# Four wide expert places become places of at most 96 tokens, computed in float32 on four 32-column quarters of the array

## The chip, the core and the metric

The kernel runs on one core of one Trainium2 chip. A core has TensorE (PE: matmuls, with weight loads listed apart as PEld), VectorE (DVE), ScalarE (ACT), GpSimd (POOL) and SyncE (SP, which here issues the transfers), each with its own instruction queue, and 16 DMA engines that bring data from HBM into the core's memory. The metric is the device time of one execution in microseconds (us). Before the change it is 1349.42 us, the median of 3 runs (1347.88 to 1350.05).

## The reference

A trunk of two layers on 256 tokens of width 1024. Each layer has a mixer (spatial gating, a recurrence and sparse attention) and a channel mixer; the first layer's channel mixer is dense, the second's has eight experts, of which each token uses two. The change touches the experts alone:

```python
def moe_swiglu(x, router_w, router_b, w1, w3, w2):
    logits = (x @ router_w + router_b).astype(jnp.float32)
    top_v, top_i = lax.top_k(logits, TOP_K)          # TOP_K = 2 of 8
    top_p = jax.nn.softmax(top_v, axis=-1)
    gate = jnp.sum(jax.nn.one_hot(top_i, N_EXPERTS) * top_p[..., None], axis=-2)
    out = jnp.zeros_like(x)
    for e in range(N_EXPERTS):
        out = out + gate[..., e:e + 1] * swiglu(x, w1[e], w3[e], w2[e])
    return out
```

with `swiglu(x, w1, w3, w2) = (silu(x @ w1) * (x @ w3)) @ w2`, w1 and w3 of 1024 x 2816, w2 of 2816 x 1024, all float32. All weights of all eight experts are read: 8 x 3 x 1024 x 2816 x 4 bytes, in 264 pieces of 1 MB.

## The kernel before

**Places.** The experts are worked through in eight places, in the order `SLOTS = "BSBBSBBS"`. The router's counts decide at run time which expert goes into which place: the three experts with the fewest tokens go to the narrow S places (at most `SCAP` = 64 tokens), the others to the wide B places (at most `CAP` = 128). The expert `FIRST` always has the first place, so that its weights can be fetched before the router has decided. Should some expert have more tokens than its place holds (`cmi` > 0), a second pass over all experts runs under `tc.If`.

**One place.** `gather` brings the tokens of two places into the core's layout by matmuls with a one-hot matrix `oh` (L1634). Then the 2816 hidden columns are done in chunks of 512 (five, and one of 256). For a chunk, `up` computes x @ w1 and x @ w3 into PSUM tiles A and B, over eight k-blocks of 128; `down` applies silu, gate and product (L1718, L1719), transposes the result (tile D, L342) and multiplies with w2 into tile O. `finish` runs a chunk's `down` after the next chunk's `up` in the program's order. After the last chunk `combine` scales O, splits it, and (every second place) adds two places' results into `h` by matmuls with `oT` and VectorE adds (L1768).

**Wide and narrow.** A B place computes in the format fp32r, where a matmul has to be split to keep the precision: each weight block `raw` is split into `hi` (ScalarE, L415) and `lo` (VectorE, L416), the tokens likewise into `mxh` and `mxl`, and a product takes three matmuls (`mm3`, L425) on the full array, 128 tokens as the stationary operand and 512 weight columns as the moving one. An S place uses plain float32 matmuls without any split, directly from `raw`: 64 tokens take half the array's columns, and two matmuls stand side by side, w1 on the one half and w3 on the other (`up_s`, L1703), or the two halves of w2's columns (`down`).

**Order and buffers.** The weights come in pieces of 1 MB (`raw`, L311) through a ring of 11 buffers (six, three and two of three pools, `ringm`, L1511). SP issues the transfers in one order, and each waits until its buffer has been read: in a B place by the splits, in an S place by the matmuls. Instructions are put in order per engine by a scheduler before the run; no engine leaves its order.

**Quarters elsewhere.** Float32 matmuls on 32-column quarters stand in the kernel already, in the compression of the attention keys (out tile A, stationary `pr`, L1049): four matmuls with different stationary blocks and different weights, 128 columns each, side by side.

Of the kernel before, what the change touches and what calls it, by code (L numbers as in the profile page):

```python
# [9 lines left out]
FP = mybir.dt.float32  # L10
# [8 lines left out]
P = 128  # L19
S = 256  # L20
# [20 lines left out]
    "GggGGGGgGgggg",  # L41
)
NE, NM, NL, NX = 6, 3, 2, 2
SLOTS = "BSBBSBBS"
FIRST = 1
SCAP = 64
EARLY = set("zs LW a eP eN eX KR Bp Kp kp kk tmp AK kr sg LI U2 L2 L4 S hs hid gc gl hr par".split())

# [18 lines left out]
def consts():  # L67
    p = np.arange(P)
    c = np.arange(P)
    same = lambda n: (p[:, None] // n) == (c[None, :] // n)  # L70
    f = {}
    f["ident"] = np.eye(P)
    f["head2"] = (p[:, None] // 64 == np.arange(2)[None, :])
    f["blk1"] = same(64)
    d = p % 64
    f["cneg"] = np.where(c[None, :] <= p[:, None], 0.0, NEG)
    f["tri"] = p[:, None] <= c[None, :]
    f["stri"] = p[:, None] < c[None, :]
# [12 lines left out]
    f["cmpn"] = np.where(ok, 0.0, NEG).reshape(P, 32)  # L91
    f["stack"] = (p % 32)[:, None] == np.arange(32)[None, :]
    f["hsel"] = (p // 16)[:, None] == np.arange(8)[None, :]
    f["iota"] = np.broadcast_to(c[None, :], (P, P))
    f["iota8"] = np.broadcast_to(np.arange(8)[None, :], (P, 8))
    f["key0"] = np.broadcast_to(np.where(np.arange(E) == FIRST, 1e6, np.arange(E))[None, :], (P, E))
    n_s = SLOTS.count("S")
    rank = {"S": iter(range(n_s)), "B": iter([E - 1] + list(range(n_s, E - 1)))}
    f["rslot"] = np.broadcast_to(np.array([next(rank[k]) for k in SLOTS])[None, :], (P, E))
    f["scan"] = np.broadcast_to((np.arange(S) % 64 != 0)[None, :], (P, S))  # L100
    inv = (1.0 / (np.float32(500000.0) ** (np.arange(0, 16, 2, dtype=np.float32) / np.float32(16)))).astype(np.float32)
    f["inv"] = np.where(d < 16, inv[d % 8], 0.0)[:, None]
    f["cm"] = (d < 16)[:, None]
    f["cm1"] = (d >= 16)[:, None]
    f["sg"] = np.where(d < 8, -1.0, np.where(d < 16, 1.0, 0.0))[:, None]
    off, o, parts = {}, 0, []
    for k in KEEP + tuple(k for k in f if k not in KEEP):
        v = f[k]
        v = np.asarray(v, np.float32)
        off[k] = (o, v.shape[1])  # L110
        o += v.shape[1]
        parts.append(v)
    return np.ascontiguousarray(np.concatenate(parts, 1)), off
# [232 lines left out]
def trunk(ctx: ExitStack, tc: tile.TileContext, A, out):  # L346
# [1257 lines left out]
    with tc.issue_after(behind):  # L1604
        quarter(0, 1)
    cap = mo.tile([P, 8], FP, name="cap")
    V.tensor_scalar(cap, rank, SLOTS.count("S") - 0.5, float(CAP - SCAP), op0=OP.is_gt, op1=OP.mult)
    V.tensor_scalar(cap, cap, float(SCAP), None, op0=OP.add)
    cmax = mo.tile([P, 1], FP, name="cmax")
    V.tensor_sub(lt[:, 0, :], cnt, cap)  # L1610
    V.tensor_reduce(cmax, lt[:, 0, :], axis=AX.X, op=OP.max)
# [22 lines left out]
    def gather(e0, kinds, pos, gate):  # L1634
# [8 lines left out]
        for e in range(2):  # L1643
            pool = late_p[0] if gathered[0] % 3 == 2 else mo2
            gathered[0] += 1
            if kinds[e] == "S":
                xs.append(pool.tile([P, 8, SCAP], FP, tag="mxh", name="xs"))
                continue
            xs.append([pool.tile([P, 8, P], FR, tag=tag, name=tag) for tag in ("mxh", "mxl")])
        for k in range(0, 8, 2):  # L1650
            for v, src in enumerate((hh_, hl_)):
                p = ps("D", (2, 2, P))
                for j in range(2):
                    for t in range(2):
                        mm(p[:, j], src[:, t, (k + j) * P:(k + j + 1) * P], oh[:, t], j == 0 and t == 0, t == 1)
                if v == 0 and k == 0:
                    first_mm.append(TE.last)
                for e in range(2):
                    if kinds[e] == "B":
                        SC.copy(xs[e][v][:, k:k + 2, :], p[:, :, e, :])  # L1660
                    elif v == 0:
                        SC.copy(xs[e][:, k:k + 2, :], p[:, :, e, :SCAP])
                    else:
                        V.tensor_add(xs[e][:, k:k + 2, :], xs[e][:, k:k + 2, :], p[:, :, e, :SCAP])
        po = ps("D", (2, 2, P))
        for t in range(2):
            for e in range(2):
# [35 lines left out]
    def up_s(st, n, x):  # L1703
# [6 lines left out]
                    mm(p[o:o + SCAP, :n], x[:, k, :], u[:, (k - k0) * n:(k - k0 + 1) * n], k == 0, k == 7)  # L1710
        return [p[0:SCAP, :n], p[SCAP:, :n]]

    dlast = []

    def down(st, kind, y, gs, n, a, b, first, last):
        w = SCAP if kind == "S" else P
        hd = mo2.tile([P, 512], FP, tag="hd", name="hd")[0:w]
        SC.activation(hd[:, :n], a, AF.Silu, scale=gs[0:w, 1:2])  # L1718
        V.tensor_mul(hd[:, :n], hd[:, :n], b)  # L1719
        nf = n // P  # L1720
        p = ps("D", (4, w))
        for f in range(nf):
            TE.transpose(p[:, f, :], hd[:, f * P:(f + 1) * P], ident[0:w, 0:w])
        if kind == "S":
            dt = mo2.tile([P, 4, SCAP], FP, tag="dh", name="ds")
            SC.copy(dt[:, :nf, :], p[:, :nf, :])
            for f in range(nf):
                u = st.next(ringm)
                for j in range(2):
# [11 lines left out]
    def combine(cell):  # L1741
# [3 lines left out]
        else:  # L1745
            if not late_p:
                spare.close()
                late_p.append(ctx.enter_context(tc.tile_pool(name="late", bufs=1, side="right")))
            yh, yl = (late_p[0].tile([P, D], FR, tag="y" + tag, name="y" + tag) for tag in ("hi", "lo"))
        for j, yj in enumerate(y):  # L1750
            s_ = slice(j * 512, (j + 1) * 512)
            SC.activation(yh[:, s_], yj, AF.Copy, scale=gs[:, 0:1])
            V.scalar_tensor_tensor(yl[:, s_], yj, gs[:, 0:1], yh[:, s_].bitcast(FP), op0=OP.mult, op1=OP.subtract)  # L1753
        if kind == "S":
            o_ = lambda j: slice(j * SCAP, (j + 1) * SCAP)
            parts = [lambda t, j, w=w: (oT[o_(j), t, :], w[o_(j), 0:512]) for w in (yh, yl)]
        else:
            parts = [lambda t, j, w=w: (oT[:, t, :], w[:, j * 512:(j + 1) * 512]) for w in (yh, yl)]
        if e % 2 == 0:
            held[:] = parts  # L1760
            return
# [10 lines left out]
    def experts(st, kinds, pos, gate):  # L1772
        prev = None
        for e, kind in enumerate(kinds):
# [4 lines left out]
            for f in range(0, DFF, NB):  # L1779
                n = min(NB, DFF - f)  # L1780
                with ExitStack() as first:
                    if first_mm[1:] == [] and e == f == 0:
                        for i in late[0], pair[0][2]:
                            first.enter_context(tc.issue_after(i))
                    a, b = (up_s if kind == "S" else up)(st, n, x)
                if prev:
                    finish(st, *prev)
                prev = (cell, n, a, b, f == 0, f + NB >= DFF)
# [26 lines left out]
    with tc.If(cv > 0):  # L1815
        V.tensor_sub(pos, pos, cap[:, None, :].to_broadcast([P, 2, 8]))
        experts(Halves(SY, A["moe"]), "B" * E, pos, gate)
        ple(1, pj, mo2, us, True, gB)


# [16 lines left out]
```

## Time and profile before

| | |
|---|---|
| time, median of 3 runs | 1349.42 us |
| the profiled execution | 1350.0 us, its span 1348.1 us |
| PE / DVE / ACT busy | 1306.3 / 890.8 / 737.4 us |
| expert stage (first matmul of the first place to the last combine) | about 603 to 1312 us of the span |
| mean granted TensorE clock | 0.986 of full speed |

The span runs from the first to the last instruction on the engines. "Busy" for PE counts matmuls whose ends are modelled, so neighbours overlap: a matmul's cost in a stream is the distance between starts, not its listed length. A line number in the profile is a line of the kernel file; matmuls all carry L339 (transposes L342), so they are told apart by the tiles they write and read.

### The profile page before, as it was taken

To read this page: it belongs to the slowest core of one execution; us is meant where nothing else is said; L and a number is where in the kernel's file an instruction comes from. 1 tells how busy PE (TensorE), PEld (TensorE's weight loads), DVE (VectorE), ACT (ScalarE), POOL (GpSimd) and SP (SyncE) were. 2 spreads that over 40 slices of the span, in tenths; PEclk is the share of its full clock that TensorE was granted. 3 is DMA by queue.
4 is the path that set the end of the run, shared out by engine and by line. 5 is a ranking of instruction groups with operands and counts; after the bars stand their busy time and mean duration, and the time that the engine had idled before them with its cause. 6 is when DMAs were issued, how large, how long until landed. Compare 5 with 4: busy or idle time off the path is not lost. (4 is left out here: it accounts for less than half of the span.)

```text
span 1348.1 us, 23186 instructions
## 1 busy us (share of the span) xinstructions
PE 1306.3 (97%) x8993; PEld 1020.9 (76%) x8993; DVE 890.8 (66%) x1452; ACT 737.4 (55%) x1161; POOL 63.3 (5%) x99
## 2 busy tenths in 40 slices
PE   8999999999999999999999999999999999999996
PEld 7998789999978898788863478888744788786345
DVE  5856876555587656878961188898622888896126
ACT  6434665444467235658851367787512777785124
POOL 3510000000000220000000000000000000000000
PEclk9899999999999999989999999999999999999998
DMA  8434046555563245466988999999999999899990
GB/s 292 126 110 160 2 134 211 190 190 189 190 217 98 86 131 187 174 246 256 372 340 366 419 419 419 377 369 358 336 380 419 419 419 419 316 386 355 416 381 34
DMA packets 64938, 367.59 MB, mean 273 GB/s; under 512 B 8254, under 2 KB 9206, under 8 KB 30518
## 3 DMA queue, kind: packets, MB, share of 16 engines
q1 hardware_dynamic: 63862, 365.13, 71.4%
q8 instruction: 72, 1.18, 0.4%
q0 software_dynamic: 960, 0.92, 0.3%
q14 instruction: 44, 0.36, 0.1%
HBM read 364.05 MB, written 1.05 MB: 271 GB/s over the span
## 5 line engine op out<-in xcount | busy, mean ns | idle before, releaser
L416 DVE TENSOR_TENSOR lo<-raw,hi 128x1024 fp32r<-128x1024 f32 x400 | 475.2, 1223 | 108.7 <-ACT hi L415 103.2
L415 ACT CAST hi<-raw 128x1024 fp32r<-128x1024 f32 x400 | 412.0, 1052 | 162.1 <-PE O L339 48.6
L339 PE MATMUL A<-raw,xs 128*64 128x512 f32 (+1 forms) x576 | 124.2, 562 | 0.0
L586 ACT CAST hi<-raw 128x512 fp32r<-128x512 f32 (+1 forms) x128 | 69.5, 594 | 79.3 <-PE zps L339 44.5
L1719 DVE TENSOR_TENSOR hd<-hd,A 64x512 f32<-64x512 f32 (+1 forms) x18 | 11.6, 645 | 140.9 <-ACT hd L1718 140.8
L587 DVE TENSOR_TENSOR lo<-raw,hi 128x512 fp32r<-128x512 f32 (+1 forms) x128 | 84.5, 692 | 22.9 <-ACT hi L586 22.5
L339 PE MATMUL O<-xl,hi 128*128 128x256 f32 x352 | 98.5, 280 | 0.1
L339 PE MATMUL O<-xh,hi 128*128 128x256 f32 x352 | 98.5, 280 | 0.0
L339 PE MATMUL O<-xh,lo 128*128 128x256 f32 x352 | 98.1, 279 | 0.0
L1718 ACT ACTIVATE hd<-A,gs 128x512 f32<-128x512 f32 (+3 forms) x48 | 31.2, 650 | 111.4 <-PE A L339 111.4
L339 PE MATMUL B<-hi,mxh 128*128 128x512 f32 (+1 forms) x240 | 90.7, 378 | 1.2 <-ACT hi L415 1.0
L339 PE MATMUL A<-lo,mxh 128*128 128x512 f32 (+1 forms) x240 | 91.1, 380 | 0.1
L339 PE MATMUL A<-hi,mxh 128*128 128x512 f32 (+1 forms) x240 | 90.9, 379 | 0.3 <-ACT hi L415 0.2
L339 PE MATMUL B<-lo,mxh 128*128 128x512 f32 (+1 forms) x240 | 90.4, 376 | 0.0
L339 PE MATMUL A<-hi,mxl 128*128 128x512 f32 (+1 forms) x240 | 89.7, 374 | 0.0
L339 PE MATMUL B<-hi,mxl 128*128 128x512 f32 (+1 forms) x240 | 89.7, 374 | 0.0
L339 PE MATMUL O<-lo,dh 128*128 128x512 f32 x220 | 88.2, 401 | 0.3 <-DVE lo L416 0.3
L339 PEld LDWEIGHTS A<-raw,xs 128*64 128x64 f32 x576 | 39.6, 136 | 64.5 <-issue 58.8
L339 PE MATMUL O<-hi,dl 128*128 128x512 f32 x220 | 86.0, 393 | 0.0
L339 PE MATMUL zps<-xh,hi 128*128 128x256 f32 x256 | 75.7, 299 | 6.6 <-DVE zr L792 5.5
L339 PE MATMUL zps<-xh,lo 128*128 128x256 f32 x256 | 73.8, 289 | 0.4 <-DVE lo L587 0.4
L339 PE MATMUL zps<-xl,hi 128*128 128x256 f32 x256 | 73.4, 288 | 0.0
(490 smaller groups left out, 2635.4 us busy)
## 6 DMA issues: line engine op xcount, KB each, us to landing
raw<-in_moe_dram SPq DMA_DIRECT2D x263, 1024.0 KB, 8.1
raw<-in_dense_dram SPq DMA_DIRECT2D x140, 512.0 KB, 3.5
raw<-in_aux_dram SPq DMA_DIRECT2D x5, 1024.0 KB, 17.2
raw<-in_dense_dram SPq DMA_DIRECT2D x8, 280.0 KB, 2.8
small<-in_small_dram SPq DMA_DIRECT2D x2, 576.0 KB, 6.0
xT<-in_xT_dram SPq DMA_DIRECT2D x2, 512.0 KB, 4.1
h<-in_x_dram SPq DMA_DIRECT2D x2, 512.0 KB, 7.7
raw<-in_moe_dram SPq DMA_DIRECT2D x2, 512.0 KB, 16.3
```

The lines of the kernel that those rows point to most:

```text
L339: self.last = self.eng.matmul(*a, **k).ins
L415: SC.copy(hi[:, :n], src)
L416: V.tensor_sub(lo[:, :n], src, hi[:, :n].bitcast(FP))
L586: SC.copy(hi[:, s_], src[:, s_])
L587: (GP if self.early else V).tensor_sub(lo[:, s_], src[:, s_], hi[:, s_].bitcast(FP))
L1718: SC.activation(hd[:, :n], a, AF.Silu, scale=gs[0:w, 1:2])
L1719: V.tensor_mul(hd[:, :n], hd[:, :n], b)
```

## The change

`SLOTS` becomes `"MSMBSMMS"`. An M place holds at most 96 tokens and computes in float32 without splits. Its 96 tokens are three blocks of 32, and 32 tokens take a quarter of the array's columns. `thirds` works on two k-blocks at a time: for each of them a round of four quarter matmuls puts the three token blocks times w1 on quarters 0 to 2 and the third token block times w3 on quarter 3 (PSUM tile `pa`); a third round puts the first two token blocks times w3 on quarters 0 and 1 for the first k-block and on quarters 2 and 3 for the second (tile `pb`). The two halves of `pb` are added afterwards (`folded`: a ScalarE copy and a VectorE sum of 64 rows). `down` does the same with the two halves of w2's columns. Experts go to places by rank: the three with the fewest tokens to S, the next three and `FIRST` to M, the one with the most to the remaining B. The pass for overflowing places gets a second repetition.

```diff
-SLOTS = "BSBBSBBS"
+SLOTS = "MSMBSMMS"
 FIRST = 1
+WIDTH = {"S": 64, "M": 96, "B": 128}
...
-    rank = {"S": iter(range(n_s)), "B": iter([E - 1] + list(range(n_s, E - 1)))}
+    rank = {"S": iter(range(n_s)), "M": iter([E - 1] + list(range(n_s, E - 2))), "B": iter([E - 2])}
...
-    V.tensor_scalar(cap, rank, SLOTS.count("S") - 0.5, float(CAP - SCAP), op0=OP.is_gt, op1=OP.mult)
-    V.tensor_scalar(cap, cap, float(SCAP), None, op0=OP.add)
+    V.tensor_scalar(cap, rank, SLOTS.count("S") - 0.5, float(WIDTH["M"] - SCAP), op0=OP.is_gt, op1=OP.mult)
+    V.tensor_scalar(lt[:, 0, :], rank, E - 2.0, float(CAP - WIDTH["M"]), op0=OP.is_equal, op1=OP.mult)
+    V.scalar_tensor_tensor(cap, cap, float(SCAP), lt[:, 0, :], op0=OP.add, op1=OP.add)
...
+    def thirds(pa, pb, x, w, first, last):
+        n = w[0][0].shape[-1]
+
+        def put(p, g, x, w, start, stop):
+            TE.matmul(p[32 * g:32 * g + 32, :n], x, w, start=start, stop=stop, tile_position=(0, 32 * g), skip_group_check=True)
+
+        for i in range(2):
+            for g in range(4):
+                put(pa, g, x[i][:, 32 * min(g, 2):32 * min(g, 2) + 32], w[i][g // 3], first and i == 0, last and i == 1)
+        for g in range(4):
+            put(pb, g, x[g // 2][:, 32 * (g % 2):32 * (g % 2) + 32], w[g // 2][1], first, last)
+
+    def up_m(st, n, x):
+        p = [ps("A", None), ps("B", None)]
+        step = 1024 // n
+        for k0 in range(0, 8, step):
+            us = [st.next(ringm) for _ in range(2)]
+            for k in range(k0, k0 + step, 2):
+                thirds(*p, [x[:, k + i, :] for i in range(2)],
+                       [[u[:, (k + i - k0) * n:(k + i - k0 + 1) * n] for u in us] for i in range(2)], k == 0, k == 6)
+        return p
+
+    def folded(a, b, n):
+        t = mo2.tile([P, 512], FP, tag="dl", name="fold")
+        SC.copy(t[0:64, :n], b[64:128, :n])
+        V.tensor_add(t[0:64, :n], t[0:64, :n], b[0:64, :n])
+        return t
...
+        if kind == "M":
+            SC.activation(hd[:, :n], a[0:w, :n], AF.Silu, scale=gs[0:w, 1:2])
+            t = folded(a, b, n)
+            V.tensor_mul(hd[64:96, :n], hd[64:96, :n], a[96:128, :n])
+            V.tensor_mul(hd[0:64, :n], hd[0:64, :n], t[0:64, :n])
...
+        if kind == "M":
+            for f in range(0, nf, 2):
+                us = [st.next(ringm) for _ in range(2)]
+                thirds(*y, [dt[:, f + i, :] for i in range(2)], [[u[:, j * 512:(j + 1) * 512] for j in range(2)] for u in us],
+                       first and f == 0, last and f == nf - 2)
+            return
...
+            if kind == "M" and j:
+                t = folded(*y, 512)
+                SC.copy(t[64:96], y[0][96:128])
+                yj = t
...
-                    a, b = (up_s if kind == "S" else up)(st, n, x)
+                    a, b = {"S": up_s, "M": up_m, "B": up}[kind](st, n, x)
...
+        V.tensor_scalar(pos, pos, float(-CAP), None, op0=OP.add)
+        experts(Halves(SY, A["moe"]), "B" * E, pos, gate)
```

The scheduler orders the new instructions anew. On PE at the start of the first place, where the gather of the first two places (D from `oh`) stands between the place's own matmuls, before (A and B are the two PSUM tiles of `up`; hi and lo the split weights, mxh and mxl the split tokens):

```order
L339 MATMUL A<-hi,mxh 128x512
L339 MATMUL B<-hi,mxh 128x512
L339 MATMUL A<-lo,mxh 128x512
L339 MATMUL D<-oh,hnh 128x256 x4
L339 MATMUL A<-hi,mxl 128x512
L339 MATMUL A<-hi,mxh 128x512
L339 MATMUL A<-lo,mxh 128x512
```

and now (xs the float32 tokens; 32 rows of output are one quarter):

```order
L340 MATMUL A<-raw,xs 32x512 x6
L340 MATMUL D<-oh,hnl 128x256 x4
L340 MATMUL A<-raw,xs 32x512 x2
L340 MATMUL B<-raw,xs 32x512 x4
L340 MATMUL A<-raw,xs 32x512
L340 MATMUL D<-oh,hnh 128x256 x4
L340 MATMUL A<-raw,xs 32x512 x7
L340 MATMUL B<-raw,xs 32x512
L340 MATMUL D<-oh,hnl 128x256 x4
L340 MATMUL A<-raw,xs 32x512 x7
L340 MATMUL D<-oh,hnh 128x256 x4
```

The gather's matmuls stood between full-array matmuls; now they cut the rounds of four. On PE in the third place, around the transposes of a chunk (D from hd), before:

```order
L339 MATMUL A<-hi,mxh 128x512
L339 MATMUL A<-lo,mxh 128x512
L339 MATMUL A<-hi,mxl 128x512
L342 MATMUL D<-ident,hd 128x128 x4
L339 MATMUL A<-hi,mxh 128x512
L339 MATMUL B<-lo,mxh 128x512
```

and now:

```order
L340 MATMUL A<-raw,xs 32x512 x8
L340 MATMUL B<-raw,xs 32x512 x4
L340 MATMUL A<-raw,xs 32x512 x8
L340 MATMUL B<-raw,xs 32x512 x4
L340 MATMUL O<-raw,ds 32x512 x24
L343 MATMUL D<-ident,hd 128x96 x4
```

The transposes of the chunk whose `up` ends there now stand behind the 24 down quarters of the chunk before. On ACT at the start of the third place, before:

```order
L415 CAST hi<-raw 128x1024 x8
L1718 ACTIVATE hd<-A,gs 128x512
L1752 ACTIVATE yhi<-O,gs 128x512
L415 CAST hi<-raw 128x1024 x4
L423 CAST dh<-D 128x512
L415 CAST hi<-raw 128x1024 x6
```

and now:

```order
L1750 ACTIVATE hd<-A,gs 96x512
L1742 COPY fold<-B 64x512
L1801 ACTIVATE yhi<-O,gs 128x512
L1763 COPY ds<-D 128x384
L1750 ACTIVATE hd<-A,gs 96x512
L1742 COPY fold<-B 64x512
```

The splits of the weights are gone from the place, and silu and the fold copy stand one behind the other.

## Rows read from the trace of the kernel before

**Rows 1.** The page's first part: busy time of each engine in us, share of the span, number of instructions.

```profile
PE 1306.3 (97%) x8993; PEld 1020.9 (76%) x8993; DVE 890.8 (66%) x1452; ACT 737.4 (55%) x1161; POOL 63.3 (5%) x99
```

**Rows 2.** Stretches of the expert stage (us from the span's start), their length, busy us of each engine with the number of instructions, the granted clock, the DMA's busy share, GB/s.

```profile
603.00:774.00 171.00, 170.75 (x826) 108.90 (x825) 92.00 (x102) 90.99 (x123) 0.00 (x0) 1.00 0.88 348
774.00:1039.00 265.00, 264.05 (x1257) 185.64 (x1256) 181.95 (x184) 159.44 (x189) 0.00 (x0) 0.99 0.98 384
1039.00:1312.00 273.00, 268.69 (x1285) 186.72 (x1284) 182.82 (x180) 161.71 (x192) 0.00 (x0) 1.00 0.97 393
```

**Rows 3.** The longest of PE's waits from 600 us to the end: who waited for whom, us in total, times, the longest.

```profile
PE D L342 <- DVE hd L1719: 1.5, 1, 1.5
PE B L339 <- ACT hi L415: 1.0, 3, 0.5
```

**Rows 4.** Timeline of PE in the first wide place (start, length in us, the matmul, its array columns and size); 37 more rows of such matmuls stand between these two.

```profile
637.31 0.39 PE L339 MATMUL A<-hi,mxh 128*128 128x512 f32 x1
...
646.01 0.39 PE L339 MATMUL B<-hi,mxh 128*128 128x512 f32 x1
```

**Rows 5.** Timeline of the weight loads in a narrow place's `down`, and the group of all its 512-column `up` matmuls (count of records; busy us, mean ns; idle before).

```profile
742.36 0.14 PEld L339 LDWEIGHTS O<-raw,ds 128*64 128x64 f32 x2 [0.29 <-issue]
742.79 0.14 PEld L339 LDWEIGHTS O<-raw,ds 128*64 128x64 f32 x2 [0.28 <-issue]
743.22 0.14 PEld L339 LDWEIGHTS O<-raw,ds 128*64 128x64 f32 x2 [0.28 <-issue]
743.65 0.14 PEld L339 LDWEIGHTS O<-raw,ds 128*64 128x64 f32 x2 [0.28 <-issue]
744.08 0.14 PEld L339 LDWEIGHTS O<-raw,ds 128*64 128x64 f32 x2 [0.29 <-issue]
...
L339 PE MATMUL A<-raw,xs 128*64 128x512 f32 x480 | 113.1, 598 | 0.0
```

**Rows 6.** Timeline of PE at the attention's quarter matmuls (32 array columns each).

```profile
107.03 1.08 PE L339 MATMUL A<-raw,pr 128*32 128x128 f32 x32
108.05 0.48 PE L339 MATMUL S<-krot,qrot 64*128 64x256 f32 x1
```

**Rows 7.** Timeline of PE where full-array matmuls and halves alternate.

```profile
701.52 0.40 PE L339 MATMUL O<-hi,dh 128*128 128x512 f32 x1
701.75 0.39 PE L339 MATMUL O<-lo,dh 128*128 128x512 f32 x1
702.08 1.08 PE L339 MATMUL A<-raw,xs 128*64 128x512 f32 x4
703.09 0.50 PE L339 MATMUL O<-hi,dl 128*128 128x512 f32 x1
```

**Rows 8.** Timeline of PE at the first matmul of the first place and at the starts of the third and the sixth (in brackets the idle time before and who ended it), and two stretches of 4 us at the third (columns as in rows 2).

```profile
603.76 0.40 PE L339 MATMUL A<-hi,mxh 128*128 128x512 f32 x1
...
773.35 0.50 PE L339 MATMUL D<-yhi,oT 128*128 128x512 f32 x1 [0.25 <-ACT gs L1676]
773.69 0.39 PE L339 MATMUL D<-ylo,oT 128*128 128x512 f32 x1
774.29 0.50 PE L339 MATMUL A<-hi,mxh 128*128 128x512 f32 x1 [0.22 <-ACT hi L415]
775.24 0.70 PE L339 MATMUL B<-hi,mxh 128*128 128x512 f32 x1 [0.44 <-ACT hi L415]
...
1039.13 0.50 PE L339 MATMUL A<-hi,mxh 128*128 128x512 f32 x1
1040.09 0.50 PE L339 MATMUL B<-hi,mxh 128*128 128x512 f32 x1 [0.45 <-ACT hi L415]
...
772.00:776.00 4.00, 3.09 (x15) 2.10 (x14) 2.60 (x6) 2.87 (x4) 0.00 (x0) 0.92 0.99 406
776.00:780.00 4.00, 4.00 (x13) 3.10 (x13) 3.72 (x4) 2.48 (x4) 0.00 (x0) 0.65 1.02 422
```

**Rows 9.** SP's longest waits for buffers from 600 us on (as rows 3), and stretches in a narrow place (1000:1020), another narrow one (740:760) and a wide one (columns as in rows 2).

```profile
SPq L311 <- DVE lo L416: 346.4, 142, 8.7
SPq L311 <- PE A L339: 73.5, 46, 4.3
...
740.00:760.00 20.00, 20.00 (x100) 7.70 (x98) 1.38 (x2) 5.16 (x13) 0.00 (x0) 1.00 1.01 418
1000.00:1020.00 20.00, 20.00 (x100) 6.82 (x98) 1.38 (x2) 2.11 (x4) 0.00 (x0) 1.00 1.01 421
1160.00:1180.00 20.00, 20.00 (x89) 15.90 (x89) 19.47 (x20) 15.47 (x16) 0.00 (x0) 1.00 0.87 325
```

**Rows 10.** Groups of ACT and DVE instructions in the expert stage (busy us, mean ns of one; idle before and who ended it).

```profile
L415 ACT CAST hi<-raw 128x1024 fp32r<-128x1024 f32 x328 | 336.8, 1052 | 70.7 <-PE A L339 28.2 <-PE O L339 21.9 <-PE B L339 12.0
L1718 ACT ACTIVATE hd<-A,gs 128x512 f32<-128x512 f32 x25 | 17.2, 687 | 12.0 <-PE A L339 12.0
L423 ACT CAST dh<-D 128x512 fp32r<-128x512 f32 x25 | 14.6, 583 | 17.1 <-PE D L342 17.1
L1718 ACT ACTIVATE hd<-A,gs 64x512 f32<-64x512 f32 x15 | 10.2, 683 | 84.8 <-PE A L339 84.8
L1726 ACT COPY ds<-D 128x256 f32<-128x256 f32 x15 | 5.5, 370 | 28.1 <-PE D L342 28.1
...
L416 DVE TENSOR_TENSOR lo<-raw,hi 128x1024 fp32r<-128x1024 f32 x330 | 389.6, 1222 | 43.5 <-ACT hi L415 38.1 <-DMA raw<-in_moe_dram 0.7
L1719 DVE TENSOR_TENSOR hd<-hd,A 64x512 f32<-64x512 f32 x15 | 10.3, 690 | 117.0 <-ACT hd L1718 117.0
```

More of the change, by code (lines that the diff above doesn't have):

```diff
@@ L1645, in gather @@
             gathered[0] += 1
-            if kinds[e] == "S":
-                xs.append(pool.tile([P, 8, SCAP], FP, tag="mxh", name="xs"))
+            if kinds[e] != "B":
+                xs.append(pool.tile([P, 8, WIDTH[kinds[e]]], FP, tag="mxh", name="xs"))
                 continue
@@ L1658, in gather @@
                 for e in range(2):
+                    w = WIDTH[kinds[e]]
                     if kinds[e] == "B":
@@ L1661, in gather @@
                     elif v == 0:
-                        SC.copy(xs[e][:, k:k + 2, :], p[:, :, e, :SCAP])
+                        SC.copy(xs[e][:, k:k + 2, :], p[:, :, e, :w])
                     else:
-                        V.tensor_add(xs[e][:, k:k + 2, :], xs[e][:, k:k + 2, :], p[:, :, e, :SCAP])
+                        V.tensor_add(xs[e][:, k:k + 2, :], xs[e][:, k:k + 2, :], p[:, :, e, :w])
         po = ps("D", (2, 2, P))
@@ L1711, in up_s @@
         return [p[0:SCAP, :n], p[SCAP:, :n]]
-    dlast = []
+    def thirds(pa, pb, x, w, first, last):
[16 more added lines that the diff above has]
+        return p
+    dlast = []
+    def folded(a, b, n):
[3 more added lines that the diff above has]
+        return t
     def down(st, kind, y, gs, n, a, b, first, last):
-        w = SCAP if kind == "S" else P
+        w = WIDTH[kind]
         hd = mo2.tile([P, 512], FP, tag="hd", name="hd")[0:w]
-        SC.activation(hd[:, :n], a, AF.Silu, scale=gs[0:w, 1:2])
-        V.tensor_mul(hd[:, :n], hd[:, :n], b)
+        if kind == "M":
[3 more added lines that the diff above has]
+            V.tensor_mul(hd[0:64, :n], hd[0:64, :n], t[0:64, :n])
+        else:
+            SC.activation(hd[:, :n], a, AF.Silu, scale=gs[0:w, 1:2])
+            V.tensor_mul(hd[:, :n], hd[:, :n], b)
         nf = n // P
@@ L1723, in down @@
             TE.transpose(p[:, f, :], hd[:, f * P:(f + 1) * P], ident[0:w, 0:w])
+        if kind != "B":
+            dt = mo2.tile([P, 4, w], FP, tag="dh", name="ds")
+            SC.copy(dt[:, :nf, :], p[:, :nf, :])
+        if kind == "M":
[4 more added lines that the diff above has]
+            return
         if kind == "S":
-            dt = mo2.tile([P, 4, SCAP], FP, tag="dh", name="ds")
-            SC.copy(dt[:, :nf, :], p[:, :nf, :])
             for f in range(nf):
@@ L1749, in combine @@
             yh, yl = (late_p[0].tile([P, D], FR, tag="y" + tag, name="y" + tag) for tag in ("hi", "lo"))
+        w_ = slice(0, WIDTH["M"] if kind == "M" else P)
         for j, yj in enumerate(y):
             s_ = slice(j * 512, (j + 1) * 512)
-            SC.activation(yh[:, s_], yj, AF.Copy, scale=gs[:, 0:1])
-            V.scalar_tensor_tensor(yl[:, s_], yj, gs[:, 0:1], yh[:, s_].bitcast(FP), op0=OP.mult, op1=OP.subtract)
+            if kind == "M" and j:
+                t = folded(*y, 512)
+                SC.copy(t[64:96], y[0][96:128])
+                yj = t
+            SC.activation(yh[w_, s_], yj[w_], AF.Copy, scale=gs[w_, 0:1])
+            V.scalar_tensor_tensor(yl[w_, s_], yj[w_], gs[w_, 0:1], yh[w_, s_].bitcast(FP), op0=OP.mult, op1=OP.subtract)
         if kind == "S":
@@ L1757, in combine @@
         else:
-            parts = [lambda t, j, w=w: (oT[:, t, :], w[:, j * 512:(j + 1) * 512]) for w in (yh, yl)]
+            parts = [lambda t, j, w=w: (oT[w_, t, :], w[w_, j * 512:(j + 1) * 512]) for w in (yh, yl)]
         if e % 2 == 0:
```

## The prediction

> **What bounds the kernel now.** I read the page first [rows 1]: TensorE (PE) is busy 97% of the span, VectorE (DVE) 66%, ScalarE (ACT) 55%. Busy PE can hide waiting, so next the list of waits in the expert stage: PE's own waits there are 1.5 us and less each [rows 3], so the stage runs at the pace at which PE gets through its matmuls. Then the stretches [rows 2]: the eight expert places take 709 of the 1348 us, with the DMA busy 0.88 to 0.98 of the time at 348 to 393 GB/s. Since stretches of one place move 421 GB/s [rows 9], the DMA is a close second bound, and it waits for buffers: SyncE's queue (SP) waits 346.4 us in all for a wide place's splits (lo, L416) and 73.5 us for a narrow place's matmuls (A, L339) [rows 9].
>
> Place lengths follow from the first matmuls of wide places [rows 8]: 603.76 to 774.29 is one wide (B) and one narrow (S) place, 170.5 us; 774.29 to 1039.13 is B, B, S, 264.8 us. So B is 94.3 and S 76.2 us, gathers and combines included.
>
> **The change, part by part.** *Rounds for triples of matmuls.* I count a place in pairs of k-blocks: five chunks of 512 hold 4 pairs each in `up`, the half chunk 4 pairs of half width, `down` 11 pairs of f-blocks: 20 + 2 + 11 = 33 full pairs. A wide place does a pair in 12 full-array matmuls. From 637.31 to 646.01 there are 38 of them, 0.229 us each [rows 4]: 2.748 us a pair. The new place does a pair in three rounds of four float32 quarter matmuls. A float32 matmul leaves two records (480 for the 240 of 512 columns in the program) [rows 5], so a round is two passes of four. What a pass of 512 columns takes the narrow places show with two halves side by side: weight loads come in twos at 742.36, 742.79, 743.22, 743.65, 744.08, 0.43 us apart [rows 5]. Four quarters side by side are in this trace too, though only 128 columns wide: 32 records, eight passes of four, fill 107.03 to 108.05 [rows 6], 1.02 us with one change of array shape in it. A quarter of 0.43 is 0.1075, and eight of those and a shape change of 0.1 are 0.96. So four do run together, with their weight loads between them, and at most (1.02/8 − 0.1075) = 0.02 us a pass on top. Bounds for a pass of 512: 0.43, if that top is fixed cost which a longer pass hides, as two halves hide it; 0.51 (4 x 0.1275), if it grows with the columns. I take 0.43, the row with the same width: a pair is 6 x 0.43 = 2.58 us, 0.168 less. Times 33 times 4 places: −22.2 us. At 0.51 it would be +41.
>
> *Broken rounds.* The first pair's gather stands between the first quarters, in runs of 6, 7, 8 and 7 quarter matmuls (first order rows) and then 6, 8 and 5. A gather matmul needs the whole array, so each run costs its most loaded quarter: 2 rounds each, 14 for 47 quarters, which full rounds would do in 11.75. 2.25 x 0.86 = +1.9 us, say +2.
>
> *Changes of array shape.* Going from full-array to halves costs 0.10 us (701.75 to 702.08 is 0.33, not 0.23), and a run of four records 1.01 instead of 0.86 [rows 7]. In the expert stage the kind of PE work (transposes, full, halves, quarters) changes 167 times before and 193 times after, counted in the programs' order. 26 more at 0.12 us: +3 us (2.6 to 3.9).
>
> *Starts of wide places after narrow ones.* There PE waits for the first splits: 0.25, 0.22 and 0.44 us at 773.35, 774.29 and 775.24, then the clock stands at half for about 3.4 us (0.92 and 0.65 in two stretches of 4 us), which loses about 1.7 us, and at 1040.09 another 0.45 [rows 8]. Both these places (third and sixth) become quarter places, which read the raw pieces. Gone: −3 us (0 to −5). What is late next is the raw piece itself; it was there before the split was.
>
> *Elementwise work.* A full chunk of a wide place has 8 + 4 splits on ACT and DVE (1052 and 1222 ns) [rows 10]; all vanish in four places, off the path, since PE hardly waits for them. New per chunk: silu on 96 rows (as 683 to 687 ns), a fold copy and a fold sum, two multiplies: by the 64-row rows (683, 690) some 2.7 us in a chain, then transposes and one copy (370 to 583 ns). Its cover: in the third place a chunk's transposes stand behind the 24 down quarters of the chunk before, 6 rounds or 5.2 us (second order rows), in the first behind the whole up of the next chunk. So 0, with 1 us for the longer chains at the places' ends, where the combine folds too (0 to 6; without cover 2.7 us at each of 24 chunks). The eviction copies of 96 columns instead of 128, and the one operation more on a 128x8 tile behind the router, lie beside gathers and DMAs: 0.
>
> *Queues.* ACT and DVE get shorter. SP issues the same pieces in the same order, but a quarter place frees a ring buffer when its matmuls have read it, not at the split some pieces earlier. Price below.
>
> Sum: −22.2 + 2 + 3 − 3 + 1 = −19.2 us. The profiled execution took 1350.0 us (span 1348.1), so 1330.8; the median of the runs shown is 0.6 below it: **1330 us**.
>
> **Rivals.** *The DMA becomes the bound.* A piece of 1 MB takes 2.50 us at 418 to 421 GB/s [rows 9]. A wide place takes 94.3/33 = 2.86 us a piece, and so refills the ring by (2.86 − 2.50) x 33/2.50 = 4.7 pieces; a narrow place (2.31) drains 2.5 by its mean, and more at its fast end. A quarter place at 94.3 − 4.8 = 89.5 us (2.71 a piece) refills 2.8. Before the second narrow place stand a quarter and a wide place, before the third two quarter places: 7.5 and 5.6 pieces against a ring of 11. For: in narrow places the DMA runs without a gap, and from 1160 to 1180 it has holes (325 GB/s) that the gain must come out of. Against: the refill still exceeds the drain. If each of the two later narrow places waits for two pieces, 4 x 2.5 = 10 us come back: 1340 us. The Trainium skill's DMA: Bandwidth & Descriptors (Specifications) gives about 358 GB/s of HBM bandwidth per core; at that a place could not fall below 33 x 2.93 = 97 us (an estimate by that page) and nothing would be won. By that figure the trace does not go: 421 GB/s over 20 us [rows 9].
>
> *The longer chains are not covered*, because ACT and DVE take their instructions in order and one placed early holds the fold back. A wait of 0.8 us at 24 chunks eats the whole gain: 1349 us. For: seven dependent steps where there were five. Against: 5.2 us of cover for 2.7.
>
> *Slower: quarters do not overlap as halves do.* If a pass of four 512-column quarters takes 0.46 to 0.51 us, as the 128-column row would have it scaled up with part or all of its excess, 792 passes (6 x 33 x 4) cost 24 to 63 us more than at 0.43: 1354 to 1393 us, middle 1370. It decides from 0.43 + 19.2/792 = 0.454 us. For: only the 128-column row has four at once. Against: of its 1.02 us some 0.1 is the shape change, and two halves of 512 columns show no excess [rows 5]. The Trainium skill speaks for this rival: TensorE: Matmul & The Clock Gate (Measured speedup vs the span model) gives 2.38 times for three column tiles and 3.07 for four row tiles. By 3.07 a round would be 4 x 0.86/3.07 = 1.12 us and the kernel some 100 us slower (an estimate by that page). Row 107.03 does not bear that out: its eight passes come far closer to four at once.
>
> *The change doesn't do what it says*: a place overflows and the second passes over all experts run. On the reference's inputs the router gives the experts 43, 68, 40, 35, 83, 113, 65 and 65 tokens: 35, 40, 43 into places of 64; 68 (the expert put first), 65, 65, 83 into 96; 113 into 128. Two more passes would each move the 264 pieces again, 264 x 2.50 = 660 us each: about 2650 us.
>
> **How the numbers follow.** Forecast 0.70, DMA 0.12, uncovered chains 0.07, slower 0.09, overflow 0.02. The forecast's own range is 1317 (the wide place's 94.3 us less the 33 x 2.748 = 90.7 of its matmuls leaves 3.6 us of losses a place, 14 in four, that may vanish too) to 1340 (shape changes at their upper price, chains +6). The 8-in-10 range takes in the DMA case and the lower part of the chains: 1317 to 1346. Within 0.2% (2.7 us, about what a measurement of this kernel tells from no change) I put half of the chains case: same 0.04, slower 0.11 (the slower and overflow cases), faster 0.85.
>
> **What would show it.** In the changed profile: A, B and O quarter matmuls (128*32) with weight loads in fours 0.43 us apart (0.454 or more: the slower rival); the third place starting some 5 us and the sixth some 11 us earlier than 774.29 and 1039.13; the clock at 1.00 throughout the quarter places; ACT and DVE far below the page's 55% and 66%; DMA above 400 GB/s in the last three places. PE waits for DMA raw would speak for the first rival, PE waits for hd or ds for the second. The forecast is wrong if the quarter places take 92 us or more each.

## The result and the profile after

The changed kernel takes 1338.17 us (median of 4 runs, 1335.75 to 1341.71) beside 1349.53 for the kernel before: a ratio of 0.991 with a 95% interval of 0.9891 to 0.9929, or 11.4 us less. A second measurement of it (after_again, below) gives 0.9925 (0.9904 to 0.9946). It is faster, as forecast, but by only some 60% of the 19.2 us that were forecast.

The profiled execution took 1335.75 us, 14.3 less than the profiled one of before. Its page, the parts that answer to [rows 1]: busy time, the granted clock and the GB/s in 40 slices, the chain that ended last by engine.

```profile
span 1334.0 us, 25800 instructions
PE 1287.9 (97%) x10673; PEld 821.2 (62%) x10673; DVE 607.0 (46%) x1233; ACT 482.5 (36%) x913; POOL 64.4 (5%) x99
PEclk8999999999999999989999999999999999999998
GB/s 295 125 111 156 11 122 221 190 190 188 190 235 95 82 124 164 165 274 214 330 340 410 419 418 419 418 418 372 339 367 420 418 419 419 320 392 393 419 391 35
PE 86%; DMA 5%; DVE 4%; ACT 3%; issue 1%; POOL 0%; SPq 0%; ACTq 0%; DVEq 0%; POOLq 0%
```

ACT and DVE fell from 55% and 66% to 36% and 46%: the splits of four places are gone. The DMA moves 418 to 420 GB/s in 10 of the slices (7 before) and has 5% of the chain.

The rounds run as the sum took them. Weight loads in the first quarter place (as [rows 5]) come in fours, 0.43 us apart, each pass of four behind the one before:

```profile
644.79 0.13 PEld L340 LDWEIGHTS A<-raw,xs 128*32 128x32 f32 x4 [0.30 <-issue]
645.22 0.13 PEld L340 LDWEIGHTS A<-raw,xs 128*32 128x32 f32 x4 [0.30 <-issue]
645.65 0.13 PEld L340 LDWEIGHTS B<-raw,xs 128*32 128x32 f32 x4 [0.30 <-issue]
646.08 0.13 PEld L340 LDWEIGHTS B<-raw,xs 128*32 128x32 f32 x4 [0.30 <-issue]
```

The place starts, as [rows 8] (PE's timeline; the last row holds the last four matmuls on expert weights):

```profile
601.84 0.64 PE L340 MATMUL A<-raw,xs 128*32 128x512 f32 x4
...
770.70 0.64 PE L340 MATMUL A<-raw,xs 128*32 128x512 f32 x4
...
1029.79 0.62 PE L340 MATMUL A<-raw,xs 128*32 128x512 f32 x2
...
1216.28 0.65 PE L340 MATMUL A<-raw,xs 128*64 128x512 f32 x2
...
1290.16 1.03 PE L340 MATMUL O<-raw,ds 128*64 128x512 f32 x4
```

The same two rows of the kernel before, for the last place (the other starts are in [rows 8]):

```profile
1236.95 0.65 PE L339 MATMUL A<-raw,xs 128*64 128x512 f32 x2
...
1305.94 1.03 PE L339 MATMUL O<-raw,ds 128*64 128x512 f32 x4
```

The borders are the first matmuls of a place, and the last of them doesn't cut the work at the same point. What is left of the seventh place's `down` behind it, after (from 1216.28 to the last four) and before (from 1237.1, where the matmul that had begun ahead of the border is done):

```profile
L340 PE MATMUL O<-raw,ds 128*32 128x512 f32 x72 | 8.1, 595 | 0.0
```

```profile
L339 PE MATMUL O<-lo,dh 128*128 128x512 f32 x6 | 2.7, 448 | 0.3 <-DVE lo L416 0.3
L339 PE MATMUL O<-hi,dl 128*128 128x512 f32 x6 | 2.3, 391 | 0.0
L339 PE MATMUL O<-hi,dh 128*128 128x512 f32 x4 | 1.4, 422 | 0.0
```

72 records are 18 passes of 0.43 us, 7.7 us; 16 full-array matmuls of 0.229 are 3.7 us. So 4.1 us more of the seventh place lie in the eighth row after the change than before it. At the other two borders the same 8 records of half-array matmuls are left in both kernels. The column "same work" moves the 4.1 us back. The forecast's terms for each stretch stand beside it (a quarter place −5.55 by its rounds and +0.75 by its share of the shape changes; +2 broken rounds in the first; by [rows 8] −2.6 at the third place's start and −0.4 at the sixth's):

| stretch | before, us | after, us | difference | same work | forecast |
|---|---|---|---|---|---|
| first and second place | 170.53 | 168.86 | −1.7 | −1.7 | −2.8 |
| third to fifth | 264.84 | 259.09 | −5.8 | −5.8 | −7.4 |
| sixth and seventh | 197.82 | 186.49 | −11.3 | **−7.2** | −10.0 |
| eighth (narrow) | 68.99 | 73.88 | +4.9 | **+0.8** | 0 |
| expert stretch, sum | 702.18 | 688.32 | −13.9 | −13.9 | −20.2, +1 for the chains |

Ahead of the expert stretch the profiled run took 1.9 us less, behind it 1.7 us more (43.84 us from the last row to the end of the span, 42.16 before). The expert stretch is the measure for the rest: in after_again it took 688.39 us (606.06 to 1294.45), 0.07 from the first profile, while the changed kernel's whole times lie 6 us apart.

In the last narrow place PE now waits for pieces of weights. Its timeline there; in brackets the idle time and who ended it:

```profile
1267.42 3.60 PE L340 MATMUL A<-raw,xs 128*64 128x512 f32 x16
1271.47 1.94 PE L340 MATMUL A<-raw,xs 128*64 128x512 f32 x8 [0.45 <-DMA raw<-in_moe_dram]
1274.05 1.94 PE L340 MATMUL O<-raw,ds 128*64 128x512 f32 x8 [0.65 <-DMA raw<-in_moe_dram]
...
1283.94 1.94 PE L340 MATMUL O<-raw,ds 128*64 128x512 f32 x8 [0.55 <-DMA raw<-in_moe_dram]
```

And two stretches of 20 us, in the seventh and in the eighth place (columns as [rows 2]), with SP's waits for ring buffers from 600 us on (as [rows 9]):

```profile
1160.00:1180.00 20.00, 20.00 (x188) 6.12 (x184) 2.06 (x3) 1.74 (x3) 0.00 (x0) 1.00 0.83 337
1260.00:1280.00 20.00, 18.39 (x92) 6.29 (x90) 1.38 (x2) 2.11 (x4) 0.00 (x0) 1.00 1.01 421
```

```profile
SPq L312 <- PE B L340: 150.0, 66, 7.1
SPq L312 <- PE O L340: 129.1, 48, 8.8
...
SPq L312 <- DVE lo L417: 75.6, 32, 4.0
```

In the seventh place the DMA idles at 337 GB/s, because SP waits for buffers that quarter matmuls have yet to read; in the eighth it runs at 421 without a break and PE still lacks pieces. SP's waits moved from the splits (lo, 346.4 us before, 75.6 now) to the matmuls (B and O, 279 us).

### The profile page after: what moved, and what is told of

The parts are those of the page before. It is cut to its first block, busy times and chain, and to the rows that moved or that the text cites. A ratio compares the mean times of both kernels' runs of the same rounds, so it can differ in the third digit from the quotient of the medians.

```text
span 1334.0 us, 25800 instructions
## 1 busy us (share of the span) xinstructions
PE 1287.9 (97%) x10673; PEld 821.2 (62%) x10673; DVE 607.0 (46%) x1233; ACT 482.5 (36%) x913; POOL 64.4 (5%) x99
## 4 chain that ended last, share of the span: by engine, by line
PE 86%; DMA 5%; DVE 4%; ACT 3%; issue 1%; POOL 0%; SPq 0%; ACTq 0%; DVEq 0%; POOLq 0%
PE O L340 24%; PE A L340 23%; PE acc L340 9%; PE B L340 9%; PE zps L340 6%; PE D L340 4%; DMA raw<-in_moe_dram 3%; PE R L340 2%; PE G L340 2%; PE D L343 2%; PE S L340 1%; PE oacc L340 1%; DMA raw<-in_dense_dram 1%; PE S L343 1%; DMA h<-in_x_dram 1%
## 5 line engine op out<-in xcount | busy, mean ns | idle before, releaser
L340 PE MATMUL A<-raw,xs 128*32 128x512 f32 (+3 forms) x2112 | 303.4, 560 | 0.7 <-DMA raw<-in_moe_dram 0.7
L417 DVE TENSOR_TENSOR lo<-raw,hi 128x1024 fp32r<-128x1024 f32 x136 | 162.8, 1222 | 71.4 <-ACT hi L416 71.4
L340 PEld LDWEIGHTS A<-raw,xs 128*32 128x32 f32 (+1 forms) x2112 | 88.3, 117 | 157.8 <-issue 141.7
L340 PE MATMUL O<-raw,ds 128*32 128x512 f32 (+1 forms) x1320 | 181.5, 595 | 2.2 <-DMA raw<-in_moe_dram 1.5
L416 ACT CAST hi<-raw 128x1024 fp32r<-128x1024 f32 x136 | 140.1, 1050 | 97.0 <-issue 40.4
L340 PEld LDWEIGHTS O<-raw,ds 128*32 128x32 f32 (+1 forms) x1320 | 50.5, 115 | 108.6 <-issue 101.4
L340 PE MATMUL B<-raw,xs 128*32 128x512 f32 (+1 forms) x768 | 105.0, 557 | 0.0
L340 PEld LDWEIGHTS O<-xl,hi 128*128 128x128 f32 x352 | 66.0, 187 | 0.4 <-DVE xl L424 0.3
L340 PEld LDWEIGHTS O<-xh,hi 128*128 128x128 f32 x352 | 66.1, 188 | 0.2
L340 PEld LDWEIGHTS O<-xh,lo 128*128 128x128 f32 x352 | 66.1, 188 | 0.0
```

Source lines behind the costliest of these rows:

```text
L340: self.last = self.eng.matmul(*a, **k).ins
L416: SC.copy(hi[:, :n], src)
L417: V.tensor_sub(lo[:, :n], src, hi[:, :n].bitcast(FP))
```

## The experiments

Each is the changed kernel with one edit, where nothing else is said. "Stretch" is the expert stretch as in the table above (the expectations count it to the last matmul, 0.4 us further: 688.8 there is 688.3 here).

**Half of the pieces** (two kernels).

```diff
-        self.todo = first[:k] + whole + first[k:]
+        self.todo = first[:k] + whole[:-2:2] + first[k:]
...
-        return [t[:, a:min(a + 1024, n)] for a in range(0, n, 1024)]
+        return [t[:, a:min(a + 1024, n)] for a in range(0, n, 1024)] * (1 if s is None else 2)
```

half_before:

> The kernel before, with every second piece of expert weights left out: each piece that arrives is used twice, so the matmuls are the same in number and order and the DMA moves half (the output is computed from half of the weights). Theory R (ring): the kernel before loses little to late pieces, 0 to 4 us below its full form. Theory G (gather, array shapes, chains): the same, 0 to 4 us. The run is the base for the next one.

half_after:

> The changed kernel with the same edit (every piece used twice, half of the weights left out). Theory R: without the shortage of pieces the whole gain on TensorE shows: 17 to 21 us below the halved kernel before, and 6 to 10 us below the full changed kernel; the last narrow place is back at 69 to 70 us from 74.3. Theory G: what is missing was lost on TensorE itself, so it is missing here too: 9 to 13 us below the halved kernel before.

Measured: 1343.19 us (ratio to the kernel before 0.996, 0.9948 to 0.9973) and 1333.19 (0.989, 0.9871 to 0.991); stretches of 698.03 and 686.30 us. So 10 us lie between the halved kernels, 11.7 in the stretch, which is what theory G said: PE waits for no piece in either, and the change still gains less than forecast, and no more than in the full kernels (13.9). One difference stands in the way of a clean reading: with pieces early, the scheduler put the instructions in another order. In the halved changed kernel the quarters are cut into 57 runs by other work, in the changed kernel into 48 (counted in the two traces). At the 0.24 to 0.32 us a cut that are read further down, nine more are 2 to 3 us (an estimate), so some 14 us would be the halved pair's gain without them.

One thing stays: behind the stretch both need the same 40.4 us, beside 42.2 and 43.8 in the full kernels. The tail's extra 1.7 us thus seems to go with the pieces; a twelfth ring buffer (ring_12 below) leaves it as it is, at 43.85 us.

**Two ring buffers more, and another order of places** (ring_more, order_alt).

```diff
-NE, NM, NL, NX = 6, 3, 2, 2
+NE, NM, NL, NX = 6, 3, 4, 2
...
-    spl[0] = ctx.enter_context(tc.tile_pool(name="splm", bufs=4))
+    spl[0] = ctx.enter_context(tc.tile_pool(name="splm", bufs=2))
```

> The changed kernel with two ring buffers more (13 in place of 11), the room taken from the split pairs of the one wide place (2 in place of 4). Theory R: 4 to 8 us faster than the changed kernel (about 1331), the last narrow place at 69 to 71 us; the wide place may lose 1 us by fewer split pairs. Theory G: within 1.5 us of the changed kernel, or slower by what the wide place loses.

```diff
-SLOTS = "MSMBSMMS"
+SLOTS = "MSMSMBMS"
```

> The changed kernel with its places in the order quarter, narrow, quarter, narrow, quarter, wide, quarter, narrow: no quarter place after a quarter place. Theory R: the ring is never full for long and never empty, so 3 to 6 us faster than the changed kernel, with the last narrow place below 72 us. Theory G: the same number of gathers, broken rounds and shape changes, so within 1.5 us of the changed kernel.

ring_more took 1358.18 us (1.0078, 1.0059 to 1.0098), a stretch of 709.17: the wide place starved for splits (PE waited 5.2 us for lo at 14 places and lost more around them). But the first two places took 166.6 us in place of 168.9 and the eighth 70.8 in place of 73.9: theory R's 4 to 8 us may be there (5.3 in these two), and are buried. order_alt took 1338.17 us (0.9928, 0.9904 to 0.9951), a stretch of 689.12, no gain: its last narrow place still takes 72.7 us. The refill arithmetic by which theory R expected 3 to 6 us is wrong.

**What a stretch of full-array work costs amid quarters** (shape_full, shape_quarter).

```diff
+        extra = lambda: mm(pw[:, 3, 96:100], ident, ident[:, 0:4])
...
+            extra()
```

> The changed kernel with 132 more matmuls of 4 columns, one behind each round of four quarters in the down part of the quarter places (33 a place); each uses the full array and writes columns that nobody reads. Theory S (array shapes): each of them costs two changes between quarters and the full array, 0.2 to 0.3 us with the matmul itself: 26 to 40 us slower than the changed kernel, and some 0.25 us between the quarters before and behind it in the trace. Theory K (the loss lies in chains, gathers or late pieces, a change of shape is about 0.03 us): 4 to 10 us slower.

For the control `extra` is

```diff
+        extra = lambda: TE.matmul(pw[0:32, 3, 96:100], ident[:, 0:32], ident[:, 0:4], start=True, stop=True, tile_position=(0, 0), skip_group_check=True)
```

> The control: the same 132 matmuls of 4 columns in the same places, on one 32-column quarter each, so that the array keeps its shape. Theory S: they cost only their own columns and the wait of one quarter, 0 to 0.06 us each: 0 to 8 us slower than the changed kernel. Theory K: the same as with the full array within 3 us.

1398.30 us (1.0345, 1.033 to 1.036) against 1343.08 (0.994, 0.9925 to 0.9954). The stretches are 747.43 and 694.65 us: 59.1 and 6.3 over 688.32, so 0.45 us for each of the 132 on the full array, 0.05 for each on a quarter. Theory S holds, at a higher price than it named. PE's timeline in shape_full, and below it the weight load of the one full-array matmul:

```profile
657.84 1.06 PE L340 MATMUL O<-raw,ds 128*32 128x512 f32 x8
658.84 0.38 PE L340 MATMUL D<-ident 128*128 128x4 f32 x2
659.15 1.06 PE L340 MATMUL O<-raw,ds 128*32 128x512 f32 x8
```

```profile
658.84 0.30 PEld L340 LDWEIGHTS D<-ident 128*128 128x128 f32 x2 [0.84 <-issue]
```

A round of 0.86 us with one such matmul takes 1.31: the quarters run out for 1.00 (0.14 more than the round), and the next quarters start 0.31 later. The Trainium skill (TensorEngine Tiling (Array Packing), Key Properties) says that changing the tiling mode, and not merely the tile, drains TensorE; the two runs agree, 0.45 against 0.05 us. They don't tell how much of the 0.45 is the change itself: the load of 128 columns of weights begins only where the quarters end and takes 0.30 us, while the control loads 32 columns in 0.11.

**Other cuts by the first gather** (gather_first).

```diff
+        last_g[:] = [TE.last]
...
-                        for i in late[0], pair[0][2]:
+                        for i in late[0], pair[0][2], last_g[0]:
```

> The changed kernel with one more condition on the first place's first chunk, by which the scheduler lets the first pair's gather cut its quarters mostly between whole rounds (runs of 6, 6, 9, 3 and then 12 quarters in place of 6, 7, 8, 7, 6, 8, 5). If broken rounds cost what the forecast booked (2 us in all), the first place is 1 to 2 us shorter and the kernel as much faster; if they cost more and explain the missing gain, 4 us or more; if nothing, 0 within 0.5 us in the trace.

1343.99 us (0.9945, 0.9933 to 0.9957), a stretch of 693.21, 4.9 longer: a miss for all three expectations, and no test of them, because the runs are now 6, 6, 9, 3, 12 and 12 quarters, which still take 14 rounds (for 48 quarters). The scheduler also put the first two transposes later, and a matmul of A waits 2.0 us for DVE's multiply (hd) ahead of it. The rows of interest are those of the cuts. In the changed kernel each of the first seven runs, of 5 to 8 quarters, takes the same 1.84 or 1.85 us, two rounds and 0.12 (three of them, with the gather's four matmuls behind each):

```profile
601.84 1.91 PE L340 MATMUL A<-raw,xs 128*32 128x512 f32 x12
603.68 0.74 PE L340 MATMUL D<-oh,hnl 128*128 128x256 f32 x4
604.36 0.62 PE L340 MATMUL A<-raw,xs 128*32 128x512 f32 x2
...
606.20 0.74 PE L340 MATMUL D<-oh,hnh 128*128 128x256 f32 x4
606.87 1.49 PE L340 MATMUL A<-raw,xs 128*32 128x512 f32 x11
...
608.72 0.74 PE L340 MATMUL D<-oh,hnl 128*128 128x256 f32 x4
```

So the forecast's 14 rounds for 47 quarters are there one by one. The gather's four matmuls take 0.67 us until the next quarter. In the kernel before, between full-array matmuls, they take 0.47 and cost nothing ahead of them:

```profile
604.23 0.40 PE L339 MATMUL A<-lo,mxh 128*128 128x512 f32 x1
604.46 0.64 PE L339 MATMUL D<-oh,hnh 128*128 128x256 f32 x4
604.93 0.40 PE L339 MATMUL A<-hi,mxl 128*128 128x512 f32 x1
```

**The ring alone, and who has room for it** (ring_12, ring_10, before_ring_12).

```diff
-NE, NM, NL, NX = 6, 3, 2, 2
+NE, NM, NL, NX = 6, 3, 3, 2
...
-    spl[0] = ctx.enter_context(tc.tile_pool(name="splm", bufs=4))
+    spl[0] = ctx.enter_context(tc.tile_pool(name="splm", bufs=3))
```

> The changed kernel with one ring buffer more (12 in place of 11) and 3 in place of 4 split pairs for the wide place. With 13 and 2 the places around lost less to late pieces (the first pair of places 166.6 us in place of 168.9, the last 71.3 in place of 74.3) but the wide place lost 20 us to its splits. If three pairs are enough for the wide place: 1 to 4 us faster than the changed kernel; if each pair missing costs alike: 6 to 10 us slower.

ring_10 has `NL` 1 and leaves the split pairs at 4:

> The changed kernel with one ring buffer less (10 in place of 11), and 4 split pairs as in the changed kernel, so that only the ring differs and the order on TensorE stays nearly the same. If late pieces in the narrow places are what the gain was lost to, as the 4.8 us won with 12 buffers say: the stretch from the first quarter to the last matmul of the last place grows from 688.8 to between 692 and 698 us, in the first and the last narrow place, with PE waits for raw pieces. If the 12 buffers won by another order of the instructions: within 1 us of 688.8.

before_ring_12 is the kernel before with ring_12's edit:

> The kernel before with the same edit as ring_12 (12 ring buffers, 3 split pairs). If late pieces cost the kernel before as much as the changed one: 3 to 6 us faster than the kernel before. If the split pairs are what its five wide places need: slower, by 1 to 10 us; then the room for the ring is something that only the change makes free.

ring_12 is the fastest kernel of the study: 1334.43 us, 0.9873 of the kernel before (0.9859 to 0.9887), 16.1 us below it in the same comparison (1350.56). Its stretch is 683.59 us, 4.7 less. PE in its last narrow place, beside the rows of after above, waits for no piece:

```profile
1267.80 7.04 PE L340 MATMUL A<-raw,xs 128*64 128x512 f32 x32
1274.67 1.89 PE L340 MATMUL O<-raw,ds 128*64 128x512 f32 x8
...
1279.89 3.62 PE L340 MATMUL A<-raw,xs 128*64 128x256 f32 x32
1283.34 1.89 PE L340 MATMUL O<-raw,ds 128*64 128x512 f32 x8
```

By its starts (605.61, 771.38, 1031.89, 1218.38, last four at 1289.20) the first two places took 165.8 us (−3.1), the third to fifth 260.5 (+1.4, of which 0.8 in the third, 0.25 in the wide place with its three split pairs and 0.35 in the fifth), the sixth and seventh 186.5 (0), the eighth 70.8 (−3.1). ring_10 took 1341.80 us (0.9941, 0.9919 to 0.9964), a stretch of 690.80, 2.5 longer, a little under the 692 expected. Its first two places took 167.8 us, 1.1 less than with 11 buffers, its eighth 76.1, with these waits in PE's list:

```profile
PE A L340 <- DMA raw<-in_moe_dram: 3.0, 6, 0.6
PE O L340 <- DMA raw<-in_moe_dram: 1.4, 3, 0.6
```

In after they are 0.7 and 1.5, in ring_12 there are none. With 10, 11 and 12 buffers the last narrow place takes 76.1, 73.9 and 70.8 us; with 13 (ring_more) 70.8 again. So the 3.1 us there are the buffer's. Those of the first two places are not shown to be: these took 167.8, 168.9, 165.8 and 166.6 us with 10 to 13 buffers, and the order of their instructions is not the same in ring_12. before_ring_12 was slower than the kernel before (1353.98 us, 1.0045, 1.0032 to 1.0058): with five wide places the fourth split pair is worth more than the twelfth buffer. Taken from there, the room is free only because the change leaves one place that splits.

**The first place wide again, and the kernel once more** (first_wide, after_again).

```diff
-SLOTS = "MSMBSMMS"
+SLOTS = "BSMBSMMS"
...
-"M": iter([E - 1] + list(range(n_s, E - 2))), "B": iter([E - 2])}
+"M": iter(range(n_s, E - 2)), "B": iter([E - 1, E - 2])}
```

> The changed kernel with its first place wide again (three quarter places). The forecast books the first place at -2.8 us (rounds -5.6, broken rounds +2, shapes +0.75): 3 us slower than the changed kernel. Theory S, by which each stretch of full-array work amid quarters loses some 0.25 us and the first place has 14 of them (8 of the gather, 6 chunks): 1 to 3 us slower. If all the gain came from the later places: 0 or faster.

> The changed kernel once more, without an edit, beside the next two: 0.989 to 0.993 of the kernel before, and a profile in which the stretch from the first quarter to the last matmul of the last place is 688 to 690 us, whatever the stage ahead of it takes.

first_wide took 1339.20 us (0.9921, 0.99 to 0.9942), a stretch of 688.65: the first quarter place is worth 0.3 us with 11 buffers, neither the 3 of the forecast nor quite the 1 of theory S. after_again: 0.9925, a stretch of 688.39.

## Why the prediction was right or wrong

**Right:** the direction, and the price of a pass. 0.43 us for four quarters of 512 columns is what the rows of narrow places gave; the rival with 0.46 to 0.51 falls. (The prediction quoted beside it the 3.07 times that the Trainium skill, TensorE: Matmul & The Clock Gate, Measured speedup vs the span model, gives for four row tiles. No run here packs row tiles; a pass of four column tiles takes the 0.43 us that two halves take [rows 5].) The broken rounds are 14 for 47 quarters, as counted. The half clock at the third place's start is gone, and with it the waits for first splits: the stretch that stood at 0.65 [rows 8] reads 1.00.

```profile
776.00:780.00 4.00, 4.00 (x44) 1.17 (x37) 0.00 (x0) 0.00 (x0) 0.00 (x0) 1.00 1.01 418
```

The longer chains cost little: PE's waits for ds, hd and yhi come to 4.7 us in all (3.2 before, from the same list).

Two of the signs failed. The third and the sixth place start 3.6 and 9.3 us earlier than before, not 5 and 11, and 1.9 of both come from ahead of the stretch; and the DMA moves 399 GB/s over the last three places, not above 400. The range's upper end of 1340 doesn't follow from the two terms named for it, which make 1336 (0.9 and 5 us above 1330).

**Wrong: the term "changes of array shape", booked at 3 us, by the rows about 10.** By these prices it is the larger part of what is missing. The forecast counted each change of the kind of work (167, then 193) and booked the 26 added ones. But transposes and gathers use the full array: between full-array matmuls they change no shape, amid quarters they change it twice. So the term wanted all such stretches in four places. Two prices can be read. A gather's four matmuls cost 0.47 us before, now 0.67 and 0.12 ahead of them. For a chunk's four transposes, PE in the third place before and the first one after:

```profile
807.24 0.63 PE L339 MATMUL O<-hi,dh 128*128 128x512 f32 x2
807.71 0.60 PE L342 MATMUL D<-ident,hd 128*128 128x128 f32 x4
808.06 0.48 PE L339 MATMUL O<-lo,dh 128*128 128x512 f32 x1
```

```profile
646.08 1.04 PE L340 MATMUL B<-raw,xs 128*32 128x512 f32 x8
647.05 0.55 PE L343 MATMUL D<-ident,hd 96*128 96x96 f32 x4
647.53 1.92 PE L340 MATMUL A<-raw,xs 128*32 128x512 f32 x16
```

0.35 us before, and the two full-array matmuls ahead end on time (0.47 for two). After, 0.48, and 0.11 ahead of it (0.97 for two passes of 0.43). That is +0.24 for a chunk's transposes and +0.32 for a gather stretch. In the changed kernel's trace 18 stretches of transposes and 17 of the gather have quarters on both sides: 18 x 0.24 + 17 x 0.32 = 9.8 us (an estimate from these rows) where 3 were booked. So this term alone was some 6.8 us too small; the stretch fell 6.3 short of the forecast's terms (the chains left out).

It shows by place too. The sixth and seventh hold nine such stretches of transposes and ten of the gather, 5.4 us where 1.5 were booked: by that price they gain 6.1 us, by the forecast 10.0, and for the same work they gained 7.2. The first place, with seven stretches of the gather, paid about 7 x 0.32 + 6 x 0.24 = 3.7 us where 0.75 was booked; with the 2 us of broken rounds that is what its rounds save (5.55), which is why first_wide loses only 0.3. And the halved kernels, with no piece late, are 11.7 us apart.

**Wrong: the claim that "the refill still exceeds the drain".** It was a balance of means for whole places, against a ring of 11 counted as if all of it were landed pieces. Its narrow place of 76.2 us is a difference of two stretches, of which the first holds two gathers and the second one. In the kernel before the fifth place starts here, and the sixth at 1039.13:

```profile
970.31 1.51 PE L339 MATMUL A<-raw,xs 128*64 128x512 f32 x6
```

That is 68.8 us for the fifth place, 2.09 a piece, and so a drain of 5.5 pieces and not 2.5, as much as the two quarter places refill (5.6). Besides, a piece now takes 12.9 us from issue to landing from 1200 us on (median of 31; 7.9 before), several are under way at once, and a quarter place holds its buffers until its matmuls have read them. So PE lacks pieces in the last narrow place: a twelfth buffer gives 3.1 us back there, and a buffer less costs 2.3 (76.14 beside 73.88). The rival "the DMA becomes the bound" named this mechanism, at 10 us; ring_12 gives 4.7 in the whole stretch. But it explains little of the shortfall. For the same work the last narrow place takes only 0.8 us more than before, since the waits that the kernel before had there are gone (1.5 us for hd [rows 3], 0.3 for lo). With the twelfth buffer the stretch is 18.6 us shorter than before; that this is close to the forecast's 19.2 is luck, a gain that the forecast didn't have against a cost that it put too low. The balance failed once more in my own test: order_alt, which never puts two quarter places in a row ahead of a narrow one, gained nothing.

**Not settled.** How the 0.24 to 0.45 us of a full-array stretch divide between the change of shape and the weight load that waits for the quarters' end. What the sixth and seventh place gained beyond that price, 1.1 us. What ring_12 won in the first two places: PE waits 1.7 us for ds there in the changed kernel and not at all in ring_12, so that another order of instructions may be the cause. And the tail's 1.7 us, which no run isolates.

## What to carry to other kernels

When work is packed into parts of the array, count every full-array helper amid it (transposes, gathers), not only the added ones: amid quarters each stretch of transposes cost 0.24 us and each of a gather 0.32 us more here than between full-array matmuls. When stretches of two kernels are compared, count the work between their borders: the scheduler moved 4.1 us of one place behind the first matmul of the next, which looked like a gain in one row and a loss in the other. When one engine gets faster and a second bound is near, a balance of means over a place isn't enough: count the buffers that are under way or held unread, and ask what the change makes free to deepen the ring. One split pair given to the ring brought 4.7 us here (3.1 of them in the place that lacked pieces), which the same edit did not bring to the kernel before.

## What the runs showed of the hardware

A 4-column float32 matmul on the full array, with its weight load, costs 0.45 us between quarter matmuls, and on a quarter 0.05 us. Four 32-column quarters of 512 float32 columns take 0.43 us a pass for a whole place, as two halves do, and a run of five quarters takes the same 1.85 us as a run of eight. And the DMA moved 419 GB/s over the 91 us of the third place, and 421 while TensorE waited for pieces in the eighth, above the 358 GB/s that the Trainium skill gives as the HBM bandwidth of a core (DMA: Bandwidth & Descriptors, Specifications), so that figure is no bound for this kernel.
